# Sparse attention's rotated queries: a switch for turning them by transposing transfers, and the shift tables of a hand-tuned order redrawn

## The chip, the cores and the metric

The kernel runs on one core of a Trainium2 chip as one program. The metric is device time in microseconds. The kernel before takes 1057.03 us in the median of three runs (1057.02 to 1057.7). Five engines work side by side, each in its own fixed order of instructions: TensorE (PE) multiplies matrices into the banks of PSUM, VectorE (DVE), ScalarE (ACT) and GpSimd (POOL) compute, SyncE (SP) issues transfers. A semaphore holds an instruction until what it reads is there and what it overwrites is free; everything behind it on the same engine waits along.

## The reference

Two layers on 256 tokens of width 1024, each with a feed-forward half-step, a mixer and a second feed-forward half-step, each followed by a layer norm. The mixer of layer 0 is a hybrid of a gated delta rule and a state-space scan; that of layer 1 is sparse attention with compressed, selected and windowed keys.

```python
def reference(x, positions, ln_g, ln_b, ffn_w_in, ffn_w_out, hyb_w_in, ...):
    h = x
    for layer in range(DEPTH):
        i = layer // 2
        h = layer_norm(DEEPNORM_ALPHA * h + 0.5 * swiglu(h, ffn_w_in[layer, 0], ffn_w_out[layer, 0]), ...)
        if layer % 2 == 0:
            mix = hybrid_mixer(h, hyb_w_in[i], ...)
        else:
            mix = nsa_mixer(h, positions, nsa_w_in[i], ...)
        h = layer_norm(DEEPNORM_ALPHA * h + mix, ln_g[layer, 1], ln_b[layer, 1])
        h = layer_norm(DEEPNORM_ALPHA * h + 0.5 * swiglu(h, ffn_w_in[layer, 1], ffn_w_out[layer, 1]), ...)
    return h
```

In the sparse attention 16 heads of width 64 stand in two groups. The compressed branch uses the queries as projected; the selected and the windowed branch use `q_rot = partial_rope(q, positions)`, the rotated queries. Each branch is a masked softmax and a sum over values; three gates mix them, and an output projection follows.

## The kernel before

The work is cut into six stages (0 feed-forward, 1 hybrid mixer, 2 and 3 feed-forward, 4 sparse attention, 5 feed-forward). In the trace they reach, by the layer norms between them, to about 178, 403, 576, 751, 870 and 1056 us. The 256 tokens are two blocks b0 and b1 of 128.

*Products.* Weights come as float32 tiles `raw` and are split into a rounded part `whi` (by ACT, `whi<-raw`) and a remainder `wlo` (by DVE, `wlo<-raw,whi`); activations likewise into two halves of a tile `x`. `mm3` (L1139) then makes three fast products of each: hi hi, hi lo, lo hi. Projections go to PSUM tag `ps` (2 banks), transposes and wide feed-forward blocks to `mp` (2 banks), sums over a whole stage to `acc` (4 banks, one for each of two blocks and two column halves). A bank is free again when its last reader, a copy by ACT or DVE, is done.

*End of a stage.* `out_terms` (L1322) adds the terms of the output projection to the four `acc` banks. At the end of a stage the last five terms go block by block: first b0's two banks, then `then(b)`, which starts b0's layer norm, then b1's. The layer norm (L1274) reads each bank with `h<-acc,h`, takes statistics, scales and shifts in two pairs (`h<-h,lnmv,lng` and `h<-h,lnve,lnb`); the result is transposed on PE (`mp<-ident,h`) into the next stage's `x`.

*Stage 4.* `queries` (L2226) projects the queries of a group and block, turns the unrotated ones by `turn` (L868): ACT copies them apart into two 16-bit halves (`words<-q`), a transposing transfer on SP's queue turns these (`turned<-words`), ACT puts them together (`qT<-turned`). Then `rope` rotates q in place and PE transposes the result into a bank of `mp` (4 transposes for each of two groups and two blocks, `mp<-ident,q`), from where it is copied and split into `qs`. In the softmax P is normalised and turned on PE as well, four transposes to a bank (`mp<-ident,P`), and copied out (`PT<-mp`, by ACT or DVE). The products with the values (`mp<-PT,vtok` and, for the compressed branch, `mp<-arena,vbd`) give the attention's output, which is copied and split into a tile `x` for the output projection.

*Stage 5.* The feed-forward's projections by token (`ps<-x,whi` and `ps<-x,wlo`) alternate between the two `ps` banks; each is evicted by ACT and DVE into `sg` (`sg<-ps`, then `sg<-ps,sg`). Wide blocks, for which sums of weights `raw<-raw,raw` are formed on DVE, stand between them on `mp`.

*What sets the order.* Nothing issues directly: the functions add operations to a plan (`Plan.add`, L394), which a list scheduler (`Plan.order`, L546) places one by one by earliest start and then by priority. The scheduler also picks the engine of copies that may run on ACT or DVE, and the buffer of each tile. The priority is the operation's place in the program plus a shift. The shifts are the table `SHIFTS` (L51): for each stage and engine a list of runs (count, shift), handed to the stage's operations of that engine in program order (end of `K.run`, L2522). All instructions bear the line of the one helper that records them, L757 (L841 after the change).

Of the kernel before, what the change touches and what calls it, by code (L numbers as in the profile page):

```python
# [14 lines left out]
AF = mybir.ActivationFunctionType  # L15
# [37 lines left out]
        "tensor": [(18, -578), (1, 84), (2, -1851), (5, 0), (2, 407), (32, 0), (11, -1907), (2, 262), (32, 0), (22, 201), (5, 382), (5, 1394),  # L53
# [4 lines left out]
        "vector": [(2, -16), (1, 0), (4, 451), (1, 4), (1, -1802), (4, 0), (1, -739), (8, 0), (1, -2831), (3, 0), (8, 275), (1, 0), (2, 22), (7, 0),  # L58
            (1, -640), (1, 0), (1, -31), (12, -213), (2, 0), (18, -135), (1, -485), (1, -700), (4, 0), (12, -453), (6, 94), (3, 16), (1, -381),
            (2, -590), (5, 31), (3, 13), (4, 0), (6, -82), (1, -177), (3, -235), (2, 378), (4, -178), (10, -583)],  # L60
        "scalar": [(3, 756), (1, 0), (6, -699), (1, -20), (4, -2184), (2, 0), (2, -327), (6, -381), (1, -2057), (3, -1945), (1, -153), (12, 82),
            (2, 328), (1, -276), (1, -88), (1, -1), (2, -105), (2, -5), (4, 0), (1, -13), (2, -258), (16, 0), (1, -130), (2, 415), (1, 361),
            (1, -453), (12, 0), (2, 37), (14, 389), (1, -116), (1, 230), (2, 204), (4, -315), (1, -74), (7, -49), (1, -67), (2, -235), (5, -23),
            (2, 0), (10, -693)],
        "gpsimd": [(1, 451), (1, 0), (1, -714), (4, -48)],
        "sync": [(6, 0), (3, -1981), (1, -3772), (6, 0), (1, -85), (5, 1078), (2, 496), (1, 0), (56, 1116)],
    },
    1: {
        "tensor": [(218, 0), (26, -298), (75, 0), (2, 188), (1, 0), (1, 70), (1, 99), (2, 0), (4, -88), (4, 228), (1, 350), (2, -643), (29, 0),
# [10 lines left out]
        "vector": [(78, 0), (10, 241), (1, 3), (5, 408), (9, 40), (18, 0), (1, 273), (2, 293), (29, -903), (3, 392), (3, 504), (2, -456), (1, -320),  # L80
# [69 lines left out]
            (6, -110), (1, 231), (3, 362), (1, -167), (7, 0), (1, 315), (35, 0), (1, -864), (26, 0), (1, 124), (5, -449), (21, 0), (7, -1270),  # L150
            (3, -1446), (2, -1431), (1, -427), (7, -479)],
        "gpsimd": [(1, 315), (5, -62), (1, 2)],
        "sync": [(20, 0), (1, -123), (20, 0), (3, -484)],
    },
}

# [33 lines left out]
def H3(t, h):  # L190
    return t.rearrange("p (h t) -> p h t", h=h)
# [2434 lines left out]
```

## Time and profile before

| what | number |
|---|---|
| median of three runs | 1057.03 us |
| the profiled execution: its own time, its span | 1058.01 us, 1056.3 us |
| PE's idle time in the span | 12.57 us |
| of it in the windows 0-178, 178-403, 403-576, 576-751, 751-870, 870-1056.3 us | 1.90, 1.62, 0.00, 0.40, 1.07, 7.58 us |
| granted PE clock over the span | 0.999 |
| transposing transfers, transposes of rotated queries on PE | 39, 16 |

Matmuls overlap in the trace: an isolated 128x512 product shows about 0.39 us, while in a run their starts are 0.23 us apart. So a product that had to wait shows less idle time in its brackets than its start was put off. DVE is nearly as full as PE over the whole span, and nearly every copy or split of the kernel queues there or on ACT.

### The profile page before, as it was taken

The page shows a single profiled execution, that of the slowest core. Times are in us where ns is not written, and L with a number is a line of the kernel's source. Part 1 is how long each engine was busy: PE and PEld are TensorE (multiplying, and loading weights), DVE is VectorE, ACT ScalarE, POOL GpSimd, SP SyncE. Part 2 cuts the span into 40 slices and gives each one's busy share as a digit, 9 for nine tenths or more (in the row PEclk, how much of TensorE's full clock was granted, in tenths as well). Part 3 has the DMA queues.
Part 4 walks back from the last instruction along what each step waited for, and adds up shares of the span by engine and source line. Part 5 has one row for each costly group of instructions (what it writes and reads, how often), then busy time and mean ns, then how long its engine had stood idle before and what let it go on. Part 6 is the DMA issues. An engine that isn't in the chain of part 4 may idle for free.

```text
span 1056.3 us, 15912 instructions
## 1 busy us (share of the span) xinstructions
PE 1043.7 (99%) x5686; PEld 868.4 (82%) x5686; DVE 1006.7 (95%) x1430; ACT 772.0 (73%) x1155; POOL 84.9 (8%) x122
## 2 busy tenths in 40 slices
PE   9999999999999999999999999999999999999997
PEld 7888888899898888888888888788887778888886
DVE  6999999898999989999999999999988999999987
ACT  7676976379867966868876678687477976878880
POOL 1001000001000201110000200000010101000100
PEclk9999999999999999999999999999999999999999
DMA  9999986744962798999779845978664355689991
GB/s 322 296 285 269 286 287 193 222 114 114 203 198 72 227 283 235 285 283 264 275 229 316 236 160 179 261 253 278 212 202 148 110 184 136 202 232 248 297 276 40
DMA packets 185977, 235.35 MB, mean 223 GB/s; under 512 B 54365, under 2 KB 115498, under 8 KB 185898
## 3 DMA queue, kind: packets, MB, share of 16 engines
q1 hardware_dynamic: 176650, 216.51, 65.1%
q0 software_dynamic: 9248, 17.83, 9.8%
q8 instruction: 45, 0.74, 0.3%
q14 instruction: 34, 0.28, 0.1%
HBM read 221.30 MB, written 1.07 MB: 211 GB/s over the span
## 4 chain that ended last, share of the span: by engine, by line
PE 52%; DVE 14%; ACT 3%; issue 3%; DMA 3%; POOL 1%; DVEq 0%; ACTq 0%; POOLq 0%
PE ps L757 18%; PE acc L757 18%; PE mp L757 15%; DVE wlo L757 5%; DMA turned<-words 2%; DVE cv L757 2%; ACT whi L757 2%; DVE arena L757 1%; DVE raw L757 1%; DVE h L757 1%; DMA G<-rates 1%; DVE qs L757 1%; DVE sw L757 0%; POOL arena L757 0%; DVE y L757 0%
## 5 line engine op out<-in xcount | busy, mean ns | idle before, releaser
L757 DVE TENSOR_TENSOR wlo<-raw,whi 128x1024 fp32r<-128x1024 f32 (+2 forms) x447 | 522.2, 1207 | 5.5 <-ACT whi L757 4.9
L757 ACT ACTIVATE whi<-raw 128x1024 fp32r<-128x1024 f32 (+1 forms) x428 | 424.0, 1044 | 53.0 <-DVE raw L757 37.3
L757 PE MATMUL ps<-whi,x 128*128 128x512 f32 (+1 forms) x544 | 144.2, 384 | 0.2 <-DVE F L757 0.2
L757 PEld LDWEIGHTS ps<-whi,x 128*128 128x128 f32 x544 | 98.2, 188 | 18.2 <-DVE x L757 0.3
L757 DVE TENSOR_TENSOR raw<-raw,raw 128x1024 f32<-128x1024 f32 x94 | 112.1, 1218 | 0.3
L757 PE MATMUL ps<-x,whi 128*128 128x512 f32 (+2 forms) x464 | 104.6, 340 | 0.7 <-ACT cv L757 0.3
L757 PE MATMUL acc<-wlo,gh 128*128 128x512 f32 x253 | 99.1, 392 | 0.2 <-DVE wlo L757 0.2
L757 PE MATMUL acc<-whi,gl 128*128 128x512 f32 x253 | 97.9, 392 | 0.0
L757 PE MATMUL acc<-whi,gh 128*128 128x512 f32 x253 | 95.9, 392 | 0.0
L757 PEld LDWEIGHTS ps<-x,whi 128*128 128x128 f32 (+1 forms) x464 | 77.6, 187 | 10.2 <-DVE cv L757 0.6
L757 PE MATMUL acc<-whi,x 128*128 128x512 f32 x256 | 82.1, 404 | 1.0 <-DVE x L757 1.0
L757 PE MATMUL mp<-whi,x 128*128 128x512 f32 x288 | 78.3, 391 | 0.0
L757 PE MATMUL ps<-wlo,x 128*128 128x512 f32 (+1 forms) x272 | 77.7, 380 | 0.0
L757 PE MATMUL mp<-whi,fhi 128*128 128x512 f32 x192 | 75.1, 391 | 0.3 <-ACT whi L757 0.3
L757 PE MATMUL mp<-whi,flo 128*128 128x512 f32 x192 | 74.8, 390 | 0.0
L757 POOL DMA_DIRECT2D raw<-in_ffn_w_in_dram x34 | 41.1, 1216 | 337.6 <-DMA raw<-in_ffn_w_in_dram 205.1
L757 PE MATMUL ps<-x,wlo 128*128 128x256 f32 (+1 forms) x344 | 66.5, 284 | 0.0
L757 PE MATMUL acc<-whi,g 128*128 128x512 f32 x192 | 63.4, 392 | 0.0
L757 PEld LDWEIGHTS mp<-whi,x 128*128 128x128 f32 x288 | 53.2, 188 | 11.7 <-ACT su L757 0.6
L757 PE MATMUL mp<-wlo,fhi 128*128 128x512 f32 x192 | 59.4, 392 | 0.1
L757 PEld LDWEIGHTS acc<-whi,x 128*128 128x128 f32 x256 | 47.8, 190 | 11.6 <-DVE x L757 1.4
L757 PEld LDWEIGHTS ps<-wlo,x 128*128 128x128 f32 x272 | 49.5, 188 | 8.7 <-DVE wlo L757 0.2
(330 smaller groups left out, 1850.3 us busy)
## 6 DMA issues: line engine op xcount, KB each, us to landing
raw<-in_ffn_w_in_dram SPq DMA_DIRECT2D x162, 512.0 KB, 6.2
raw<-in_ffn_w_out_dram SPq DMA_DIRECT2D x88, 512.0 KB, 6.1
raw<-in_hyb_w_in_dram SPq DMA_DIRECT2D x44, 512.0 KB, 5.4
raw<-in_ffn_w_in_dram POOLq DMA_DIRECT2D x34, 512.0 KB, 9.1
raw<-in_ffn_w_in_dram SPq DMA_DIRECT2D x52, 256.0 KB, 4.7
raw<-in_hyb_w_out_dram SPq DMA_DIRECT2D x16, 512.0 KB, 4.4
raw<-in_nsa_w_in_dram SPq DMA_DIRECT2D x10, 512.0 KB, 5.4
raw<-in_nsa_cmp_w_dram SPq DMA_DIRECT2D x8, 512.0 KB, 3.9
```

The lines of the kernel that those rows point to most:

```text
L757: r = getattr(getattr(nc, eng), fn)(*[res(a) for a in args], **{k: res(a) for k, a in kw.items()})
```

## The change

New switches are added: `R_TURN` for turning the rotated queries by transfers instead of on PE, `P_TURN` for doing so with P, and `H_BANKS` for the bank tags of some projections. `turn` takes a list of sources as well. The tables in `SHIFTS` are replaced, for all six stages; they now hold more and shorter runs. All entries of `R_TURN` and `P_TURN` are 0, and those of `H_BANKS` name the tag that stood there before.

```diff
+R_TURN = (0, 0, 0, 0)
+P_TURN = (0,) * 24
+H_BANKS = ('ps', 'ps', 'ps', 'ps', 'ps', 'ps')
...
     def turn(self, out, src):
-        n = src.ids.size // P
+        n = out.ids.size // P
...
-        self.nc.scalar.activation(w, src.words(), AF.Copy)
+        parts = src if isinstance(src, list) else [src]
+        k = n // len(parts)
+        for j, part in enumerate(parts):
+            self.nc.scalar.activation(w[:, :, j * k:(j + 1) * k], part.words(), AF.Copy)
...
                 self.rope(H3(q[b][:, gs], 8), b, 8)
                 yield
-                pt = self.bank("mp")
-                for c in range(4):
-                    nc.tensor.transpose(pt[:, c * P:(c + 1) * P], q[b][:, g * 512 + c * P:g * 512 + (c + 1) * P], self.ident)
+                if R_TURN[2 * g + b]:
+                    pt = self.m4(512, "qr", "H")
+                    self.turn(H3(pt, 4), H3(q[b][:, gs], 4))
+                else:
+                    pt = self.bank("mp")
+                    for c in range(4):
+                        nc.tensor.transpose(pt[:, c * P:(c + 1) * P], q[b][:, g * 512 + c * P:g * 512 + (c + 1) * P], self.ident)
...
-                        self.copy(dst, pt)
+                        if P_TURN[g * 12 + half * 2 + r + (4 + half * 2 + r + kb if b else 0)]:
+                            self.turn(H3(dst, 4), [t[:, :, r, ks] for t in tiles])
+                        else:
+                            pt = self.bank("mp")
+                            for n in range(4):
+                                nc.tensor.transpose(pt[:, n * P:(n + 1) * P], tiles[n // nh][:, n % nh, r, ks], self.ident)
+                            self.copy(dst, pt)
```

The tables are long; these are the first runs of stage 5's PE table, new. Each pair is a count of instructions and the number added to the priority of each.

```diff
+        "tensor": [(45, 0), (1, 632), (4, 380), (3, 358), (1, 376), (8, 612), (34, 0), (1, 176), (1, 28), (10, 0), (3, 26), (15, 0), (12, 76),
```

The counts of stage 4's PE table sum to 671 before and to 655 now; the stage has 671 PE operations in both kernels. Stage 5's sums to 735 before (the rest has no shift) and to 777 now, all that the stage has.

The kernels hold the same instructions, apart from a few copies and splits whose engine the scheduler picks: 5233 on PE, 488 transfers issued by SP, 39 of them transposing, and PE's 16 transposes `mp<-ident,q`. The order differs from PE's row 145 on. PE's instructions stand by 2 to 7 rows elsewhere on average in stages 0 to 3, by 16 (at most 120) in stage 4 and by 11 (at most 95) in stage 5. Three places follow; the numbers in names tell tiles apart and differ between the kernels.

**The end of stage 4, PE.** Before, from the last product of the attention (`vbd`) on; x_1573 is the attention's output, acc_1630 and acc_1638 are b1's banks:

```order
L757 MATMUL mp_1676_9018<-arena_1486_7885,vbd_1557_8305 64x128 x8
L757 MATMUL acc_1630_8754<-wlo_1616_8674,x_1573_8407 128x512
L757 MATMUL acc_1630_8754<-whi_1600_8581,x_1573_8407 128x512
L757 MATMUL acc_1638_8824<-whi_1600_8581,x_1573_8407 128x512
L757 MATMUL acc_1638_8824<-wlo_1616_8674,x_1573_8407 128x512
L757 MATMUL acc_1638_8824<-whi_1600_8581,x_1573_8407 128x512
L757 MATMUL acc_1638_8824<-whi_1610_8616,x_1573_8407 128x512
L757 MATMUL acc_1638_8824<-wlo_1620_8690,x_1573_8407 128x512
L757 MATMUL acc_1630_8754<-whi_1610_8616,x_1573_8407 128x512
```

Now, from the same place; x_1581 is the attention's output, acc_1625 a bank of b0, acc_1621 and acc_1623 are b1's:

```order
L841 MATMUL mp_1676_9021<-PT_1671_9004,vtok_1468_7764 64x512
L841 MATMUL mp_1676_9021<-arena_1485_7882,vbd_1558_8319 64x128 x8
L841 MATMUL acc_1625_8736<-wlo_1639_8803,x_1581_8448 128x512
L841 MATMUL acc_1625_8736<-whi_1635_8792,x_1581_8448 128x512
L841 MATMUL acc_1621_8701<-whi_1587_8477,x_1581_8448 128x512
L841 MATMUL acc_1621_8701<-wlo_1591_8510,x_1581_8448 128x512
L841 MATMUL acc_1623_8710<-whi_1587_8477,x_1581_8448 128x512
L841 MATMUL acc_1623_8710<-wlo_1591_8510,x_1581_8448 128x512
```

Before, b0's last products stood ahead of the block of PT,vtok products that ends with `vbd`, and five products that read older parts of x stand between `vbd` and the first reader of the new part (whi_1610). Now b0's last two products come behind `vbd`, and the one after them (whi_1587) reads the new part.

**The end of stage 4, DVE.** Before, from b0's second read of its banks on; here ACT makes the first copy into x:

```order
L757 SCALAR_TENSOR_TENSOR h0_1661_8962<-acc_1609_8614,h0_1443_7633 128x512
L757 TENSOR_TENSOR wlo_1678_9025<-raw_1595_8553,whi_1673_9009 128x1024
L757 TENSOR_TENSOR wlo_1680_9032<-raw_1617_8676,whi_1677_9020 128x1024
L757 BN_STATS lnst_1664_8972<-h0_1661_8962 128x6
L757 BN_AGGR lnmv_1682_9045<-lnst_1664_8972 128x2
L757 TENSOR_SCALAR lnve_1683_9049<-lnmv_1682_9045 128x1
L757 SCALAR_TENSOR_TENSOR h0_1661_8962<-h0_1661_8962,lnmv_1682_9045,lng_1656_8931 128x512 x2
L757 TENSOR_TENSOR x_1573_8407<-mp_1676_9018,x_1573_8407 128x4x128
L757 SCALAR_TENSOR_TENSOR h0_1661_8962<-h0_1661_8962,lnve_1683_9049,lnb_1658_8937 128x512 x2
```

Now, from two splits ahead of the copy, which is a CAST on DVE:

```order
L841 TENSOR_TENSOR wlo_1681_9034<-raw_1579_8436,whi_1677_9024 128x1024
L841 TENSOR_TENSOR wlo_1683_9041<-raw_1592_8512,whi_1680_9032 128x1024
L841 CAST x_1581_8448<-mp_1676_9021 128x4x128
L841 SCALAR_TENSOR_TENSOR h0_1668_8994<-acc_1625_8736,h0_1443_7633 128x512
L841 TENSOR_TENSOR x_1581_8448<-mp_1676_9021,x_1581_8448 128x4x128
L841 BN_STATS lnst_1672_9007<-h0_1668_8994 128x6
L841 BN_AGGR lnmv_1686_9069<-lnst_1672_9007 128x2
L841 TENSOR_SCALAR lnve_1687_9072<-lnmv_1686_9069 128x1
L841 SCALAR_TENSOR_TENSOR h0_1668_8994<-h0_1668_8994,lnmv_1686_9069,lng_1658_8933 128x512 x2
L841 SCALAR_TENSOR_TENSOR h0_1668_8994<-h0_1668_8994,lnve_1687_9072,lnb_1659_8936 128x512 x2
```

The second read of b0's bank has moved from ahead of two splits to behind the CAST, the statistics come behind both conversions of x, and the conversion that stood between the two pairs of b0's layer norm is gone from there.

**Stage 5, the two ps banks.** PE before, from the last product of the projection ps_1737 to the first of ps_1757, two projections on:

```order
L757 MATMUL ps_1737_9345<-x_1694_9105,wlo_1729_9304 128x256
L757 MATMUL ps_1754_9422<-x_1694_9105,whi_1714_9248 128x512
L757 MATMUL mp_1743_9374<-whi_1744_9376,fhi_1711_9232 128x512
L757 MATMUL mp_1743_9374<-whi_1744_9376,flo_1712_9240 128x512
L757 MATMUL mp_1743_9374<-whi_1744_9376,fhi_1711_9232 128x512
L757 MATMUL mp_1743_9374<-whi_1744_9376,flo_1712_9240 128x512
L757 MATMUL mp_1743_9374<-wlo_1750_9405,fhi_1711_9232 128x512 x2
L757 MATMUL mp_1743_9374<-whi_1746_9385,fhi_1711_9232 128x512
L757 MATMUL mp_1743_9374<-whi_1746_9385,flo_1712_9240 128x512
L757 MATMUL ps_1757_9441<-x_1694_9105,whi_1721_9273 128x512
```

PE now, around the last products of ps_1751 and the first of ps_1759:

```order
L841 MATMUL ps_1751_9415<-x_1695_9110,wlo_1719_9266 128x256 x2
L841 MATMUL ps_1751_9415<-x_1695_9110,wlo_1722_9277 128x256 x3
L841 MATMUL mp_1734_9319<-wlo_1754_9435,fhi_1711_9233 128x512 x2
L841 MATMUL mp_1734_9319<-whi_1755_9441,fhi_1711_9233 128x512
L841 MATMUL mp_1734_9319<-whi_1755_9441,flo_1714_9244 128x512
L841 MATMUL mp_1734_9319<-whi_1755_9441,fhi_1711_9233 128x512
L841 MATMUL mp_1734_9319<-whi_1755_9441,flo_1714_9244 128x512
L841 MATMUL ps_1751_9415<-x_1695_9110,wlo_1722_9277 128x256
L841 MATMUL mp_1734_9319<-wlo_1756_9452,fhi_1711_9233 128x512 x2
L841 MATMUL ps_1759_9468<-x_1695_9110,whi_1724_9283 128x512 x4
```

DVE now, at the same place; ps_1747 is the projection before ps_1751 (its last product is 17 PE rows above that of ps_1751):

```order
L841 TENSOR_TENSOR wlo_1756_9452<-raw_1694_9106,whi_1755_9441 128x1024
L841 TENSOR_TENSOR raw_1704_9155<-raw_1704_9155,raw_1694_9106 128x1024
L841 TENSOR_TENSOR sg_1757_9460<-ps_1751_9415,sg_1757_9460 128x256
L841 TENSOR_TENSOR raw_1684_9043<-raw_1684_9043,raw_1726_9290 128x1024
L841 TENSOR_TENSOR raw_1694_9106<-raw_1694_9106,raw_1730_9303 128x1024
L841 TENSOR_TENSOR sg_1749_9401<-ps_1747_9375,sg_1749_9401 128x256
L841 TENSOR_TENSOR wlo_1762_9489<-raw_1684_9043,whi_1760_9476 128x1024
```

The new order evicts ps_1751 ahead of ps_1747, and ps_1759 starts two products behind the last one of ps_1751; before, nine products stood between a projection's end and the start of the one that takes its bank.

**Stage 4, the transposes of P.** Four of them fill a bank. PE before, for one half of b1's heads:

```order
L757 MATMUL mp_1586_8497<-ident_7_284,P_1567_8372 128x128 x2
L757 MATMUL mp_1586_8497<-ident_7_284,P_1571_8393 128x128 x2
L757 MATMUL ps_1581_8456<-whi_1526_8153,x_1454_7692 128x512
L757 MATMUL ps_1581_8456<-wlo_1529_8172,x_1454_7692 128x512
L757 MATMUL ps_1581_8456<-whi_1526_8153,x_1454_7692 128x512
L757 MATMUL ps_1581_8456<-whi_1531_8185,x_1454_7692 128x512
L757 MATMUL ps_1581_8456<-wlo_1534_8199,x_1454_7692 128x512
L757 MATMUL ps_1581_8456<-whi_1531_8185,x_1454_7692 128x512
L757 MATMUL mp_1587_8516<-ident_7_284,P_1567_8372 128x128 x2
L757 MATMUL mp_1587_8516<-ident_7_284,P_1571_8393 128x128 x2
L757 MATMUL mp_1588_8524<-ident_7_284,P_1567_8372 128x128 x2
L757 MATMUL mp_1588_8524<-ident_7_284,P_1571_8393 128x128 x2
```

PE now, for the same:

```order
L841 MATMUL ps_1583_8462<-kd1_1502_7979,qs01_1576_8422 128x256
L841 MATMUL mp_1595_8528<-ident_7_284,P_1577_8431 128x128
L841 MATMUL mp_1596_8531<-ident_7_284,P_1577_8431 128x128
L841 MATMUL mp_1595_8528<-ident_7_284,P_1577_8431 128x128
L841 MATMUL mp_1595_8528<-ident_7_284,P_1584_8465 128x128 x2
L841 MATMUL mp_1596_8531<-ident_7_284,P_1577_8431 128x128
L841 MATMUL mp_1596_8531<-ident_7_284,P_1584_8465 128x128 x2
L841 MATMUL mp_1600_8555<-ident_7_284,P_1577_8431 128x128 x2
L841 MATMUL mp_1600_8555<-ident_7_284,P_1584_8465 128x128 x2
L841 MATMUL mp_1602_8562<-ident_7_284,P_1577_8431 128x128 x2
L841 MATMUL mp_1602_8562<-ident_7_284,P_1584_8465 128x128 x2
L841 MATMUL ps_1604_8574<-kd0_1496_7958,qs01_1576_8422 128x256
```

Before, products of a projection (ps_1581) stand between the second group of four and the third, as further up between the first and the second; now sixteen transposes stand in a row.

More of the change, by code (lines that the diff above doesn't have):

```diff
@@ L61 @@
[L61 to L65, printed above, removed]
@@ new lines @@
+    3: {
+        "tensor": [(1, 3), (1, 4), (4, 0), (18, 7), (2, 76), (3, 0), (1, 6), (1, 21), (1, 22), (8, 24), (2, 39), (1, 0), (1, 41), (6, 0), (2, 70),
[9 rows of a table added]
+        "vector": [(1, -40), (2, -64), (2, 0), (1, 21), (1, 33), (2, 43), (5, 0), (1, 74), (1, 93), (1, -53), (1, 0), (1, -10), (1, 9), (1, 0),
[6 rows of a table added]
+        "scalar": [(6, -110), (2, 0), (2, 32), (1, 47), (1, 72), (1, -46), (1, -43), (2, 83), (1, 0), (1, 81), (1, 0), (1, -29), (1, -104), (1, -98),
[6 rows of a table added]
+        "gpsimd": [(1, -178), (1, -166)],
+        "sync": [(2, -213), (1, -205), (1, -211), (1, -205), (1, -202), (3, 0), (3, -164), (4, -161), (1, -266), (2, -265), (1, 0), (1, -278),
+            (1, -275), (1, 0), (1, -265), (2, -252), (4, -235), (2, -258), (4, 0), (2, -110), (2, -116), (1, -101), (6, 91), (2, -80), (1, -68),
+            (2, 0), (1, -78), (5, -68), (4, 0), (1, -85), (1, -71), (1, -91), (2, -89), (6, 0), (1, -55), (1, -29), (2, -28), (3, 0), (3, -106),
+            (1, -14)],
+    },
@@ new lines @@
+    5: {
+        "tensor": [(45, 0), (1, 632), (4, 380), (3, 358), (1, 376), (8, 612), (34, 0), (1, 176), (1, 28), (10, 0), (3, 26), (15, 0), (12, 76),
[7 rows of a table added]
+        "vector": [(1, 30), (6, 0), (1, 1), (1, 23), (1, 0), (1, 832), (2, 1013), (3, 0), (1, 103), (1, 143), (2, -31), (1, 16), (1, 176), (1, 122),
[4 rows of a table added]
+        "scalar": [(9, 3), (1, 400), (1, 106), (1, 430), (1, 0), (3, 1471), (1, -6), (8, 0), (1, -3), (5, 0), (2, -236), (4, 27), (3, 284),
+            (3, -171), (1, 116), (10, 0), (1, -450), (2, -603), (1, -607), (3, -192), (1, 281), (1, 182), (4, 0), (1, -210), (3, 0), (1, -11),
+            (2, -82), (1, -16), (41, 38), (1, 0), (1, 286), (1, 266), (3, 28), (9, -29), (1, 456), (4, 378), (7, 0), (2, 7), (2, 189), (2, 0),
+            (4, -57)],
+        "gpsimd": [(1, 65), (2, -278), (3, 315), (1, 81), (5, -183)],
+        "sync": [(1, 0), (27, 51), (4, -104), (4, -257), (6, 0), (1, -93), (2, -24), (5, 0), (1, -11), (1, 0), (1, 380), (1, 381), (20, 0), (1, 280),
+            (5, 214), (10, -57)],
@@ L1604, in z_gate_steps @@
             for b in range(2):
-                ps = self.bank("ps")
+                ps = self.bank(H_BANKS[4 + b])
                 for k in range(KD):
@@ L1961, in space @@
             vT = [H3(self.m4(1024, f"vT{n}"), 4) for n in range(2)]
-            yield from gdn_conv("v", [(8 + n, vT[n // 4][:, n % 4, :]) for n in range(8)])
+            yield from gdn_conv("v", [(8 + n, vT[n // 4][:, n % 4, :]) for n in range(8)], H_BANKS[:2])
             for b, d in enumerate(blk):
@@ L1992, in space @@
                     w = ws[0][e] if ws else self.these("x", self.unit_cols, w_in, 4112 + c * P, P)[0]
-                    ps = self.bank("ps")
+                    ps = self.bank(H_BANKS[2 + e])
                     yield from self.two_steps(x, w, ps)
@@ L2440, in attend @@
                 for r in range(2):
-                    tq = None
                     for kb in range(b + 1):
                         yield
-                        pt = self.bank("mp")
-                        for n in range(4):
-                            nc.tensor.transpose(pt[:, n * P:(n + 1) * P], tiles[n // nh][:, n % nh, r, kb * P:(kb + 1) * P], self.ident)
-                        if b == 0:
-                            if r == 0:
-                                tl = self.m4(1024, "PT", "Q")
-                            dst = tl[:, r * 512:(r + 1) * 512]
-                        else:
-                            if kb == 0:
-                                tl = self.m4(1024, "PT", "Q")
-                            dst = tl[:, kb * 512:(kb + 1) * 512]
-                        self.copy(dst, pt)
+                        ks = slice(kb * P, (kb + 1) * P)
+                        if b == 0 and r == 0 or b and kb == 0:
+                            tl = self.m4(1024, "PT", "Q")
+                        o = (kb if b else r) * 512
+                        dst = tl[:, o:o + 512]
+                        if P_TURN[g * 12 + half * 2 + r + (4 + half * 2 + r + kb if b else 0)]:
+                            self.turn(H3(dst, 4), [t[:, :, r, ks] for t in tiles])
+                        else:
+                            pt = self.bank("mp")
+                            for n in range(4):
+                                nc.tensor.transpose(pt[:, n * P:(n + 1) * P], tiles[n // nh][:, n % nh, r, ks], self.ident)
+                            self.copy(dst, pt)
                         PT[half, r, kb] = dst
```

61 lines of the change are left out of this document (25 added, 36 removed), and 180 rows, old and new, of the table SHIFTS.

## The prediction, made before the change was run

> **What bounds the kernel now.** I read the page's span and busy shares first, then the windows by stage, then the rows of TensorE's timeline that carry a wait. The page:
>
> ```profile
> span 1056.3 us, 15912 instructions
> ...
> PE 1043.7 (99%) x5686; PEld 868.4 (82%) x5686; DVE 1006.7 (95%) x1430; ACT 772.0 (73%) x1155; POOL 84.9 (8%) x122
> ```
>
> TensorE (PE) is the bound, with VectorE (DVE) close behind: an eviction or a layer norm that has to queue on DVE finds it busy 95% of the time. The windows, one row for a stage (stage 1, the hybrid mixer; stage 4, sparse attention; stage 5, the last feed-forward), say where PE has idle time:
>
> ```profile
> core 0: us, PE busy (x) PEld busy (x) DVE busy (x) ACT busy (x) POOL busy (x), PEclk, DMA share, GB/s
> 178.00:403.00 225.00, 223.38 (x1714) 197.43 (x1713) 210.45 (x431) 164.65 (x273) 18.55 (x28) 1.00 0.66 185
> 751.00:870.00 119.00, 117.93 (x782) 93.53 (x781) 110.71 (x228) 90.00 (x246) 13.80 (x27) 1.00 0.52 161
> 870.00:1056.30 186.30, 178.72 (x819) 147.55 (x818) 174.02 (x200) 129.42 (x156) 14.81 (x14) 0.99 0.74 206
> sum 1056.30, PE 1043.73 PEld 868.42 DVE 1006.65 ACT 772.04 POOL 84.90; mean PE 173.96 PEld 144.74 DVE 167.78 ACT 128.67 POOL 14.15
> ```
>
> PE idles 1056.30 - 1043.73 = 12.6 us. Of this 186.30 - 178.72 = 7.6 lie in stage 5, and nearly all of that behind PE's last product:
>
> ```profile
> 291.93 2.05 PE L757 MATMUL acc<-X,AT 64*64 64x32 f32 x64 [0.47 <-DVE X L757]
> ...
> 788.20 1.06 PE L757 MATMUL mp<-ident,P 128*128 128x128 f32 x8 [0.30 <-DVE P L757]
> ...
> 840.69 0.66 PE L757 MATMUL mp<-ident,P 128*128 128x128 f32 x4 [0.48 <-DVE arena L757]
> ...
> 1048.65 0.28 PE L757 MATMUL mp<-whi,gl 128*128 128x256 f32 x1
> ```
>
> That product starts at 1048.65 and the span ends at 1056.3, a tail whose order the change leaves as it is. Stage 1 idles 1.6 us and stage 4 1.1 us; the rows above the last (in brackets the idle time and who ended it) show the largest waits. Only work that PE no longer waits for, or new waits, can move the end, since its products are the same before and after: **everything is won or lost in waits of some tenths of a microsecond.** About 4 us of waits lie before the tail, some 6 if I add 0.16 to each, because products overlap (0.39 us each, started 0.23 apart, as a row below shows).
>
> **What the change is.** In its words the rotated queries are turned by transfers. The new switch for it, R_TURN, is zero in all four places. The order rows show PE with 16 transposes of q after the rope as before, and 39 transposing transfers both times. So what runs is the same work in another order: the SHIFTS tables are redrawn, in all six stages. Were the switches on, these rows would price it:
>
> ```profile
> L757 PE MATMUL mp<-ident,q 128*128 128x128 f32 x16 | 2.6, 275 | 0.0
> ...
> L757 ACT ACTIVATE words<-q 128x1024 uint16<-128x1024 uint16 x4 | 4.3, 1078 | 0.1
> ...
> L757 ACT ACTIVATE qT<-turned 128x1024 uint16<-128x1024 uint16 x4 | 5.5, 1380 | 0.0
> ```
>
> PE would lose at most 2.6 us and ScalarE (ACT) gain 4.3 + 5.5 = 9.8. They are off, so I cost this at 0. But stage 4's new table counts 655 of PE's instructions, sixteen fewer than the 671 that the stage has and that the old table counts. Behind the first of the sixteen transposes its numbers fall on instructions up to sixteen places off. I read it as numbers drawn for the form with the switches on. Stages 0 to 3 and 5 have tables that fit.
>
> **Term A, end of stage 4: +1.2 us (0 to 2.3).** Here is how the stage ended before:
>
> ```profile
> 868.05 1.04 PE L757 MATMUL mp<-arena,vbd 128*64 128x128 f32 x16
> 869.02 0.50 PE L757 MATMUL acc<-wlo,x 128*128 128x512 f32 x1
> ...
> 873.65 1.04 PE L757 MATMUL mp<-ident,h 128*128 128x128 f32 x8
> ```
> ```profile
> 869.14 0.60 ACT L757 ACTIVATE x<-mp 128x512 fp32r<-128x512 f32 x1 [3.45 <-PE mp L757]
> ```
> ```profile
> 868.14 0.69 DVE L757 BATCH_NORM_STATS2 lnst<-h 128x6 f32<-128x512 f32 x1
> ...
> 869.17 1.41 DVE L757 SCALAR_TENSOR_TENSOR h<-h,lnmv,lng 128x512 f32<-128x512 f32 x2
> 870.50 0.69 DVE L757 TENSOR_TENSOR x<-mp,x 128x512 fp32r<-128x512 f32 x1
> 871.10 1.41 DVE L757 SCALAR_TENSOR_TENSOR h<-h,lnve,lnb 128x512 f32<-128x512 f32 x2
> 872.42 1.22 DVE L757 TENSOR_TENSOR wlo<-raw,whi 128x1024 fp32r<-128x1024 f32 x1
> ```
>
> After the last attention product (vbd, 868.05) five products that need no new input cover the copy of its result into x: the copy ends at 869.14 + 0.60 = 869.74, and the sixth product starts at about 869.02 + 5 x 0.23 = 870.2. The h0 transposes at 873.65 find h ready (872.5). In the new order two products stand between vbd and the first reader of x, the copy is a DVE cast behind four weight splits (1.22 each), and b0's last product, which h0 <- acc waits for, comes after vbd and no longer before the 3.5 us of PT,vtok products. With DVE free at 869.14 the cast ends at 869.83 against a reader at 869.48: with a hand-off about 0.5 of wait. The second half of x (DVE third in line, 0.60 apart) is done near 871.05, its reader due near 870.9: 0.2. Layer norm goes on for 0.7 + 0.25 + 1.4 + 1.4 (statistics, small operations, two pairs) to 874.7, the first transposes at PE's thirteenth product after that are due at 874.0 and want the first half, near 874.2: 0.2. The next stage's x then has its two conversions with less PE work beside them: 0.3. Sum 1.2. If the cast has to wait out one split the first term grows by 1.1; if x is free early, nothing of this shows.
>
> **Term B, stage 5, the two ps banks: +0.85 us (0 to 2).** The eviction of one projection takes an ACT and a DVE step:
>
> ```profile
> 900.66 0.39 ACT L757 ACTIVATE sg<-ps 128x256 f32<-128x256 f32 x1 [1.13 <-PE ps L757]
> ```
> ```profile
> 901.20 0.42 DVE L757 TENSOR_TENSOR sg<-ps,sg 128x256 f32<-128x256 f32 x1
> ```
> ```profile
> 902.32 2.00 PE L757 MATMUL ps<-x,whi 128*128 128x512 f32 x8
> ```
>
> From ACT's start to DVE's end it is 901.62 - 900.66 = 0.96 us; products start (2.00 - 0.39) / 7 = 0.23 apart. In the new DVE order the eviction of ps_1747, long complete, stands behind that of ps_1751, so the projection ps_1759 takes the bank of ps_1751, whose last product lies two products (0.46) ahead of it. 0.28 for that product plus 0.96 and hand-offs, less 0.12 + 0.46, is 0.75; a raw <- raw of about 1.2 us ahead on DVE may add: 0.85. Before, nine products stood at that place. Later ps_1810 meets the same with its su <- ps copy two products ahead: +0.4 (0 to 0.6).
>
> **Term C, transposes of P: +0.9 us (0 to 1.2).** The copies out of the two mp banks, and the densest stretch of these transposes now:
>
> ```profile
> L757 ACT ACTIVATE PT<-mp 128x512 f32<-128x512 f32 x16 | 9.1, 598 | 2.0 <-PE mp L757 1.8
> ```
> ```profile
> 860.18 1.03 PE L757 MATMUL mp<-ident,P 128*128 128x128 f32 x8
> 860.97 0.71 PE L757 MATMUL acc<-whi,x 128*128 128x512 f32 x2
> ...
> 861.75 1.04 PE L757 MATMUL mp<-ident,P 128*128 128x128 f32 x8
> ```
>
> Eight transposes fill both banks in 0.8 us and 0.78 us of products follow, as long as a copy. The new order puts sixteen in a row: the third four needs the first bank back, three transposes (0.33) after it was filled, against 0.27 + 0.60 (somewhat more where DVE copies) and hand-offs; the fourth four waits for the other copy. About 0.6 + 0.3.
>
> **What goes: -1.8 us (-6 to 0).** The eight transposes at 788.20 now stand in fours with two other rows between: the 0.30 there (0.46 by starts) goes. Of the rest of stage 4 I let as much go again, and 0.9 of stages 1 to 3, whose tables are now drawn in finer runs. Their waits (0.47 at 291.93 the largest) hang on chains of ACT and DVE that the order can cover but not shorten.
>
> **Queueing that I can't place: +1.4 us (0 to 7).** In stage 4 PE's rows move by 16 places on average, up to 120, with numbers meant for other instructions, and DVE there is at 110.71 of 119 us. No row prices a misplaced eviction before it happens. The nearest is stage 4's own 1.1 us of idle time (some 1.6 with overlaps), so I take about that; the upper end is five such stretches.
>
> **Sum:** 1.2 + 0.85 + 0.4 + 0.9 - 1.8 + 1.4 = +2.95. The profiled execution took 1058.01 (span 1056.3 and 1.7 around it) and would become 1060.96. The median shown is 1057.03, about 1 us below it; the same step gives **1060.0**.
>
> **Rivals.** (1) *The new waits are paid by old ones* (28%): A to C are covered because DVE runs ahead of PE there, and the sum stays within 2.1 us, 1055 to 1059. For it speaks that 4 us of idle time is small anyway; against it that each place has two products of cover where five to nine stood. (2) *Faster* (16%): the finer tables of stages 1 to 3 take away the waits on X, cv and x, and stage 4 those at 788 and 840. It decides where A to C cost under 1.5 together while over 4 of the 6 us go: 1053 to 1054.9. (3) *Stage 4's table out of step costs much* (11%): each of its 24 PT copies or 16 softmax blocks late by 0.4 gives 6 to 10 us, 1063 to 1067. (4) *The clock* (1%): the windows show PEclk 1.00 in every stage but the last, whose 0.99 holds the idle tail; 0.01 more of 186.3 us would cost 1.9 us, giving 1062. The Trainium skill ("TensorE: Matmul & The Clock Gate", section "A second HAM failure mode: psum-queue depth-cycling") says that short idle times between groups of products that cycle through PSUM banks can swing the clock between half and full. By that rule terms B and C could cost more than their waits; the waits at 788 and 840 lie in a window with 1.00 granted, so the trace so far speaks against it. That the change turns the queries by transfers has no chance of its own, since the rows of the new order still hold the transposes.
>
> **How the numbers follow.** Forecast +2.1 to +6: 44%. With (3) and (4) that makes slower 56%, within 0.2% (2.1 us, what a measurement of this kernel can tell from no change) 28%, faster 16%. The range leaves out about a tenth at each side: half of (2)'s gain at the low end, 1054.5, and most of (3) at the high, 1066.5.
>
> **What would show it.** A: brackets on acc <- whi,x just behind mp <- arena,vbd, and on mp <- ident,h. B: a bracket on ps <- x,whi near 905 to 920 naming sg. C: sixteen mp <- ident,P with brackets naming PT. Queueing: PE's idle time in stage 4's window above 1.1 us by more than A and C. I am wrong if stage 4 and 5 together idle no more than now, or if stages 1 to 3 give back over 2 us.

## The result, and the profile after

The changed kernel takes 1071.72 us in the median of four runs (1069.73 to 1075.82), before 1057.37 (1057.02 to 1058.4): **1.0143 of the time before, 95% interval 1.0127 to 1.0159.** Slower, as forecast, but by some 14 us and not by 3, and above the range's upper end of 1066.5. The profiled execution was the slowest of its runs, 1075.82 us. Its page:

```profile
span 1074.1 us, 15926 instructions
PE 1050.9 (98%) x5686; PEld 870.8 (81%) x5686; DVE 1008.2 (94%) x1425; ACT 772.1 (72%) x1158; POOL 85.7 (8%) x124
```

The work is the same; PE is busy 7 us longer for it, and idle for longer. To show where, the windows below run between three marks: the last transposes of h (`mp<-ident,h` of b1) behind stage 3, those behind stage 4, and PE's last product. Columns as in the prediction: bounds, length, busy time of PE, PEld, DVE, ACT, POOL, granted clock. Before:

```profile
0.00:764.40 764.40, 760.48 (x4173) 639.37 (x4173) 735.29 (x1026) 558.47 (x765) 58.14 (x84) 1.00 0.79 236
764.40:885.80 121.40, 120.33 (x775) 94.43 (x774) 111.88 (x227) 92.82 (x248) 15.28 (x28) 1.00 0.52 161
885.80:1048.70 162.90, 162.69 (x744) 134.60 (x742) 155.07 (x169) 120.75 (x144) 10.55 (x10) 1.00 0.77 212
```

After, and below it three short windows in it:

```profile
0.00:769.00 769.00, 762.95 (x4188) 642.43 (x4189) 736.35 (x1027) 562.24 (x772) 59.89 (x84) 1.00 0.79 235
769.00:895.70 126.70, 120.42 (x760) 93.95 (x758) 110.97 (x221) 90.19 (x243) 11.96 (x28) 0.97 0.45 142
895.70:1066.50 170.80, 167.27 (x744) 134.43 (x741) 156.69 (x169) 119.70 (x144) 12.97 (x11) 0.99 0.73 213
830.10:836.90 6.80, 5.84 (x28) 5.85 (x28) 5.97 (x13) 5.30 (x13) 2.72 (x7) 0.50 0.20 39
301.10:304.50 3.40, 3.40 (x9) 2.64 (x9) 3.27 (x7) 1.36 (x2) 0.25 (x1) 0.50 0.40 139
939.30:942.70 3.40, 3.40 (x8) 2.72 (x9) 3.40 (x5) 3.40 (x5) 0.91 (x1) 0.51 1.11 217
```

Stages 0 to 3 end 4.6 us later, stage 4 takes 5.3 more, stage 5 7.9 more; the tail is 7.6 us both times. By cause: PE's idle time ahead of its last product was 3.9 + 1.1 + 0.2 = 5.2 us and is 6.1 + 6.3 + 3.5 = 15.9, so 10.7 more. And PE was granted half its clock for 3.4, 6.8 and 3.4 us, which before did not happen ahead of the tail; half of 13.6 us is 6.8 us of work lost at most (PE was idle for 1 us of them, which both sums count). 10.7 + 6.8 = 17.5 of the 17.8 us by which the span grew. (In the rows for single stages some work has moved over a mark.)

The largest single loss, in PE's timeline:

```profile
824.73 0.28 PE L841 MATMUL ps<-kd,qs 128*128 128x256 f32 x1
828.28 0.44 PE L841 MATMUL mp<-ident,P 128*128 128x128 f32 x2 [3.27 <-ACT P L841]
829.07 0.88 PE L841 MATMUL mp<-ident,P 128*128 128x128 f32 x6 [0.35 <-ACT P L841]
831.06 1.97 PE L841 MATMUL mp<-ident,P 128*128 128x128 f32 x8 [1.11 <-DVE PT L841]
```

These are the sixteen transposes of term C. Their brackets sum to 4.7 us, and the half clock of the window at 830.1 follows: eight transposes that took 1.03 us at 860.18 before take 1.97. ACT's timeline in the same stretch:

```profile
823.41 0.50 ACT L841 ACTIVATE P<-acc,arena 128x256 f32<-128x256 f32 x1
...
827.00 0.55 ACT L841 ACTIVATE P<-acc,arena 128x256 f32<-128x256 f32 x1
...
827.64 3.43 ACT L841 ACTIVATE P<-P,arena 128x256 f32<-128x256 f32 x8
```

ACT does sixteen exponentials (some 0.45 us apart, the last ten in a row, a short accumulator read with each), and only then normalises P (`P<-P`), which PE wants. Before, at the same place, ACT normalised the first half's P ahead of the last four exponentials, and the transposes of P stood between projections (`ps<-whi,x` and `ps<-wlo,x`):

```profile
816.88 1.77 ACT L757 ACTIVATE P<-P,arena 128x256 f32<-128x256 f32 x4
818.48 0.54 ACT L757 ACTIVATE P<-acc,arena 128x256 f32<-128x256 f32 x1
```
```profile
818.39 0.49 PE L757 MATMUL mp<-ident,P 128*128 128x128 f32 x3
...
820.57 0.60 PE L757 MATMUL mp<-ident,P 128*128 128x128 f32 x4
...
822.41 1.32 PE L757 MATMUL mp<-ident,P 128*128 128x128 f32 x8
```

DVE, in the changed kernel, shows no idle time from 823 to 833 us. The copy that gives the second eight transposes their bank stands behind its own queue:

```profile
826.92 1.22 DVE L841 TENSOR_TENSOR P<-P,arena 128x1024 f32<-128x1024 f32 x1
...
829.18 1.22 DVE L841 TENSOR_TENSOR wlo<-raw,whi 128x1024 fp32r<-128x1024 f32 x1
830.32 0.68 DVE L841 COPY PT<-mp 128x512 f32<-128x512 f32 x1
```

So the wait of 3.27 us is PE's longest, but with DVE's order as it is the second eight would have waited without it too: the chain of work that ended last runs through DVE here, not through ACT. Terms A and B left these rows:

```profile
879.24 1.02 PE L841 MATMUL acc<-whi,x 128*128 128x512 f32 x2
...
880.56 0.40 PE L841 MATMUL acc<-wlo,x 128*128 128x512 f32 x1
881.02 0.73 PE L841 MATMUL acc<-whi,x 128*128 128x512 f32 x2
...
884.13 0.63 PE L841 MATMUL mp<-ident,h 128*128 128x128 f32 x4
...
927.26 2.11 PE L841 MATMUL ps<-x,whi 128*128 128x512 f32 x8 [0.73 <-DVE sg L841]
...
937.82 1.19 PE L841 MATMUL acc<-whi,g 128*128 128x512 f32 x4 [1.44 <-ACT whi L841]
...
956.78 0.50 PE L841 MATMUL ps<-whi,fhi 128*128 128x512 f32 x1 [0.23 <-ACT su L841]
```

A: two products in 1.02 where two in a row take 0.62, and a start 0.23 late at 881.02; none at the transposes of h. B: 0.73 on sg, and 0.23 on su. The 1.44 on `whi` at 937.82 stood in no term.

### The profile page after: what moved, and what is told of

The parts are those of the page before. It is cut to its first block, busy times and chain, and to the rows that moved or that the text cites. A ratio compares the mean times of both kernels' runs of the same rounds, so it can differ in the third digit from the quotient of the medians.

```text
span 1074.1 us, 15926 instructions
## 1 busy us (share of the span) xinstructions
PE 1050.9 (98%) x5686; PEld 870.8 (81%) x5686; DVE 1008.2 (94%) x1425; ACT 772.1 (72%) x1158; POOL 85.7 (8%) x124
## 4 chain that ended last, share of the span: by engine, by line
PE 54%; DVE 4%; DMA 2%; ACT 1%; issue 1%; POOL 0%; DVEq 0%; ACTq 0%; POOLq 0%
PE ps L841 19%; PE acc L841 19%; PE mp L841 17%; DMA raw<-in_ffn_w_in_dram 2%; ACT whi L841 1%; DVE arena L841 1%; DVE raw L841 1%; DVE wlo L841 0%; DVE qs L841 0%; DVE h L841 0%; DVE x L841 0%; POOL lnve L841 0%; DVE F L841 0%; DVE vg L841 0%; DVE P L841 0%
```

## The experiments

The theories, of which C took shape on the way: **M**, the loss is a table out of step, since its numbers fall on other instructions than they were drawn for; **L**, it is the sum of separate places; **C**, a table holds only for the whole schedule that it was drawn with; **K**, lost clock that follows from waits. Times are medians, ratios to the kernel before on the same chip with their intervals.

### Whole tables exchanged

Six of these seven kernels take one or more stages' entries of `SHIFTS` from before; three set the switch.

```diff
 SHIFTS = {
...
-    4: {"tensor": [...], ...},    # new
+    4: {"tensor": [...], ...},    # of before
...
-R_TURN = (0, 0, 0, 0)
+R_TURN = (1, 1, 1, 1)
```

Stage 4's table of before:

> The changed kernel with stage 4's table of before (PE, DVE, ACT, POOL, SP lists), all else as changed. Theory L (the loss is local: in the profile of the changed kernel stage 4 holds waits of 3.3, 0.35 and 1.1 us on the transposes of P at 828 to 831 us and then 6.8 us at half clock, worth 4.7 + 3.4 = 8 us; stage 5 holds waits of its own): 1071.7 - 8, so 1062 to 1066, with stage 5's waits near 927 and 938 still there. Rival H (stage 5's waits are handed over from stage 4's bad end): both go, 1056 to 1059.

Stage 5's:

> The changed kernel with stage 5's table of before, all else as changed. Theory L: stage 5 gives back its waits (some 3.5 us of brackets between 927 and 959) and the 1.7 us that its 3.4 us at half clock cost, so 1065 to 1068, with the wait on ACT's P at about 828 and the half clock behind it unchanged. Rival H: stage 5's waits stay or come elsewhere, 1070 to 1073.

Both:

> The changed kernel with the tables of before in stages 4 and 5: what is left of the change is the new tables of stages 0 to 3 alone. Theory L: no half clock before the tail and the stages 1 to 3 as in the changed kernel, which reach the same point 4.6 us later than before in its profile (1.7 of it half clock at 301): 1058 to 1062. Rival S (stages 0 to 3 gained by their finer tables, the profile's shift is only work moved over a stage's border): 1053 to 1057.

All tables new and the switch on:

> The changed kernel with R_TURN = (1, 1, 1, 1): the rotated queries are turned by four more transfers, as the change's words say, PE has 16 transposes fewer, ACT eight copies more, and stage 4's table of 655 PE entries fits its 655 instructions. Theory M (the loss in stage 4 comes from a table that is out of step): the wait before the transposes of P and the half clock go, 1060 to 1064. Rival O (the order of the table is bad for the chip by itself: sixteen transposes of P still stand in a row there): the wait stays, 1068 to 1073.

The next three expectations were written with the results of these four known. The switch on, stages 0 to 3 of before:

> The changed kernel with R_TURN = (1, 1, 1, 1) and the tables of before in stages 0 to 3: the turning by transfers and the new tables of stages 4 and 5 alone, which is what the change's words say. Adding up by stages (before's 764.4 us to the end of stage 3, then 118.9 + 163.5 + 7.8 us as in x4_turn_on): a span of 1054.6, a time of 1056, within 0.2% of before. Theory C (a stage's table holds only behind the stages it was drawn behind): stage 4 and 5 take 10 us or more longer, 1066 or more.

The switch on, all tables of before:

> The changed kernel with R_TURN = (1, 1, 1, 1) and all tables of before: the turning by transfers by itself, with nothing redrawn. By its work alone (2.6 us less on PE at most, 9.8 us more on ACT): 1055 to 1060. Theory C: the old table of stage 4 meets other instructions, 1066 to 1090.

The switch off, stages 0 to 3 of before:

> The changed kernel (R_TURN 0) with the tables of before in stages 0 to 3: the new tables of stages 4 and 5 alone. If the loss belongs to these two tables without the turning, as in the changed kernel: stage 4 about 126, stage 5 about 170 us, 1067 to 1073. Theory C in its strong form (every mix comes out differently): outside of that, either way.

Measured (the last three columns from the marks described above, in each profile):

| kernel | tables 0-3, 4, 5; turns | time, us | ratio | end of stage 3 | stage 4 | stage 5 |
|---|---|---|---|---|---|---|
| before | old, old, old; off | 1057.3 | 1 | 764.4 | 121.4 | 162.9 |
| changed | new, new, new; off | 1071.7 | 1.0143 (1.0127 to 1.0159) | 769.0 | 126.7 | 170.8 |
| x4 | new, new, new; **on** | 1059.2 | 1.0017 (1.0007 to 1.0026) | 767.6 | 118.9 | 163.5 |
| x2 | new, new, old; off | 1066.8 | 1.0086 (1.0058 to 1.0114) | 769.3 | 125.3 | 163.1 |
| x8 | old, new, new; on | 1079.2 | 1.0195 (1.0180 to 1.0210) | 766.1 | 132.7 | 169.9 |
| x1 | new, old, new; off | 1085.6 | 1.0290 (1.0247 to 1.0332) | 762.9 | 137.6 | 174.7 |
| x10 | old, new, new; off | 1088.2 | 1.0284 (1.0267 to 1.0301) | 767.2 | 134.9 | 174.8 |
| x3 | new, old, old; off | 1091.8 | 1.0325 (1.0307 to 1.0343) | 767.4 | 135.1 | 180.5 |
| x9 | old, old, old; on | 1095.5 | 1.0354 (1.0339 to 1.0370) | 762.5 | 155.8 | 167.4 |

With the switch on, as the change's words have it, the new tables give almost the time of before, 0.17% above it: with all four turns on PE gone (2.6 us of busy time at most) nothing is won, but 12 us of loss do not come either. Stage 4 then takes 118.9 us. This is a little better than theory M asked for (1060 to 1064), and since the code is the same but for the switch, it shows that the loss comes from running these tables without the transfers. (The changed code with all tables of before and the switch off was not run.) **Theory L falls.** The very table of stage 4 that gives 121.4 us behind the old stages 0 to 3 gives 135.1 and 137.6 behind the new ones (x3, x1), and the new one that gives 118.9 behind new stages gives 132.7 behind the old (x8). x8 is the clearest: by adding up stages it should have taken 1056 us, and it takes 1079. My expectations for x1 and x3 (1062 to 1066, 1058 to 1062) were off by some 20 and 30 us for that reason; x9 and x10 came out above the 1066 to 1090 of theory C and the 1067 to 1073 of adding up. One mix goes against the strong form of C: x2, where stage 5's old table behind the new stage 4 takes 163.1 us, as at home, and gives back 7.7 us of the changed kernel's profile; its time of 1066.8 us lies in the 1065 to 1068 that theory L had named. So stage 5's loss hangs on its table and not on a bad hand-over alone.

### The same number for the same instruction

```diff
+                    self.turned.append(len(self.plan.ops))
                     for c in range(4):
                         nc.tensor.transpose(...)
...
-                mine = iter([op for op in ops if op.eng == eng])
+                mine = []
+                for op in ops:
+                    if op.idx in self.turned:
+                        mine += [None] * {"scalar": 2, "sync": 1}.get(eng, 0)
+                    if op.eng == eng and not any(0 <= op.idx - k < 4 for k in self.turned):
+                        mine.append(op)
```

> The changed kernel with R_TURN still 0, but stage 4's table handed out as if it were 1: the sixteen transposes of rotated queries on PE take no entry, and where the transfers would stand ACT passes over two entries and SP over one, so that every other instruction gets the number that it has with the turns on. Theory M (a number for the wrong instruction is what costs): 1060 to 1064, no wait of 3 us ahead of the transposes of P, no half clock near 830. Rival C (the table holds only for the whole schedule it was drawn with, so that the transposes on PE and their PSUM banks are enough to upset it): 1066 to 1073, with waits of over 3 us in sum in stage 4.

1076.23 us, ratio 1.0175 (1.0151 to 1.0199), stage 4 127.9 us, stage 5 171.0. **Theory M falls too**, though I had built the forecast's reading of the table on it. Every instruction but the sixteen transposes, which have no shift, has the number drawn for it, and the kernel is no faster than the changed one. So what the table misses is not its place in the list. That it misses the transfers themselves follows from x4: with four transposes for each block on PE and a bank of `mp` between, the scheduler puts out another order. Whether shifts of their own for the sixteen transposes would mend it was not tried. The profile shows the 3.3 us at P gone and others in their place (DVE on PT 2.3 us in four waits, ACT on PT 1.2, ACT on P 0.9 in stage 4), and half clock for 3.41 us at 828.7 and again at 839.0. Theory C's sum of over 3 us came; its time, 1066 to 1073, was too low.

How the same place looks in x4, PE's timeline:

```profile
824.57 0.87 PE L841 MATMUL mp<-ident,P 128*128 128x128 f32 x6 [0.36 <-ACT P L841]
826.10 1.43 PE L841 MATMUL mp<-ident,P 128*128 128x128 f32 x8 [0.66 <-ACT PT L841]
828.08 1.26 PE L841 MATMUL mp<-ident,P 128*128 128x128 f32 x8 [0.54 <-DVE PT L841]
```

There too sixteen transposes stand in a row, and more. The second and third eight wait 0.66 and 0.54 us for their banks, 1.2 in sum, near the 0.9 of term C; but the scores whose exponentials P needs start at 810.3, 42.7 us into the stage, with projections between them until 821.7. In the changed kernel their first part comes at 44.5 us, but the last eight products start at 52.3 to 55.4, the last projection starts at 54.6 and the last product of all at 55.7, and from 56.0 to 59.3 PE has nothing to do.

### What the wait at P consists of

```diff
+        early = {6537, 6538, 6539, 6540}      # P<-P of the first half, on ACT
+        moved = [x for i, x in zip(placed, order) if i in early]
+        at = placed.index(6536) + 1           # behind the reciprocal's product
+        return order[:at] + moved + [x for i, x in zip(placed[at:], order[at:]) if i not in early]
```

> The changed kernel with four instructions moved on ACT alone: the normalising of the first half's P (P <- P, four), which in the changed order stands behind the eight exponentials of the second half, goes to right behind the reciprocal that it needs, ahead of the last four of these exponentials. In the profile of the changed kernel the reciprocal's product is done at 825.86 us and the first of the four starts at 827.64. Theory E (the 3.3 us that PE waits there are ACT's order: the transposes of P wait for ACT, not for their PSUM banks): that wait falls to some 1.5 us, the time by 1.5 to 4 us (what the half clock behind it gives back included), so 1068 to 1071 where x13_again gives about 1072 to 1073. Rival F (the banks, or DVE's share of the normalising, or ACT's total work are late next, as I had priced it): the wait only moves to the next transposes, within 1 us of x13_again.

> The changed kernel on the same chip, beside x12_scale_first: 1070 to 1075, with the wait of 3.3 us at about 828.

x12 takes 1074.16 us, ratio 1.0159 (1.0134 to 1.0184), the changed kernel beside it 1071.68, ratio 1.0130 (1.0112 to 1.0149): no gain, so E's 1068 to 1071 is missed, and by the medians 2.5 us more where F said within 1, with intervals that overlap. PE in x12, and DVE:

```profile
824.35 0.44 PE L846 MATMUL mp<-ident,P 128*128 128x128 f32 x2 [1.49 <-ACT P L846]
...
826.02 0.76 PE L846 MATMUL mp<-ident,P 128*128 128x128 f32 x5 [0.54 <-DVE P L846]
830.55 1.97 PE L846 MATMUL mp<-ident,P 128*128 128x128 f32 x8 [3.76 <-DVE PT L846]
```
```profile
827.53 0.28 DVE L846 TENSOR_TENSOR arena<-arena,arena 128x120 f32<-128x120 f32 x1 [1.56 <-ACT arena L846]
...
828.67 1.22 DVE L846 TENSOR_TENSOR wlo<-raw,whi 128x1024 fp32r<-128x1024 f32 x1
829.80 0.69 DVE L846 COPY PT<-mp 128x512 f32<-128x512 f32 x1
```

Both theories had a half of it. The wait on ACT's P falls from 3.27 to 1.49 us, where E said 1.5, so that wait was ACT's order (the four now stand ahead of the last four exponentials, as they do before). But the next eight transposes then wait 3.76 us for the copy out of their bank, as F said: that copy stands on DVE behind a product that waits 1.56 us for ACT (`arena`, behind the exponentials moved back), a cast and a split. From the end of stage 3 to the second eight transposes it is 63.7 us in x12 and 62.1 in x13. The four instructions were in the wrong place, and a better place for them alone is worth nothing here, because DVE's queue holds the next transposes all the same.

### The clock

```diff
+            if op.idx == 6542:                # the first of the sixteen transposes
+                pt, (_, kd, qs) = args[0].t.view(), ops[6708].args[:3]
+                order += [("tensor", "matmul", (pt[:, :256], kd, qs), dict(start=True, stop=True))] * 26
```

> The changed kernel with 26 products more (128x256, kd by qs, into the PSUM bank that the transposes of P overwrite next; 26 x 0.12 = 3.1 us) where PE waits 3.3 us for P. Theory K (the 6.8 us at half clock behind 830 us follow from PE's idle time, and cost 3.4 us by themselves): no half clock there or 3.4 us of it only, 1.7 to 3.4 us faster than the changed kernel, 1068 to 1070, though PE has more to do. Rival N (the half clock has another cause): the half clock stays, 1071 to 1073.

> As x6_fill_products, with 28 transposes of the identity (128x128, 28 x 0.11 = 3.1 us) in place of the products. If transposes count as work for the clock as products do: as there, 1068 to 1070. If they don't: the half clock at 830 stays, 1071 to 1073.

x6 takes 1072.03 us (1071.03 to 1073.07), ratio 1.0141 (1.0121 to 1.0161); x6b 1074.39, ratio 1.0157 (1.0132 to 1.0181) (1072.28 to 1074.57 in three executions; a fourth ran at 0.555 of the clock from end to end, took 1753.79, and is the one that was profiled). x6's profile:

```profile
824.36 3.27 PE L844 MATMUL mp<-kd,qs 128*128 128x256 f32 x26
827.80 0.44 PE L844 MATMUL mp<-ident,P 128*128 128x128 f32 x2 [0.17 <-ACT P L844]
828.59 0.88 PE L844 MATMUL mp<-ident,P 128*128 128x128 f32 x6 [0.35 <-ACT P L844]
830.58 1.97 PE L844 MATMUL mp<-ident,P 128*128 128x128 f32 x8 [1.11 <-DVE PT L844]
```

With the gap filled the half clock comes still, but for 3.41 us (830.5 to 833.9) where the changed kernel has 6.83 in three profiles. That much is in K's words; but the time, 1072.0, is in rival N's range and not in K's, and stage 4's 125.6 us stand beside 125.8 to 126.7 in the changed kernel's three profiles. Nor did the filling take all idle time away: 0.17 + 0.35 + 1.11 = 1.6 us of waits are left just ahead of the half clock. So x6 doesn't decide between K and N, and x6b doesn't either; what ties the half clock to idle time is the count over all profiles in the last section.

The changed kernel once more:

> The changed kernel once more, five rounds, for the clock: its time less the time lost to the granted clock (one minus the mean clock, times the span). Theory K: its runs differ by the number of 3.4 us episodes at half clock, so that the time less the lost time is steadier, 1063 to 1068, while the lost time goes from 4 to 10 us; before loses about 2 us, all of it behind PE's last product. Rival: the lost time is as in before, and the runs differ by waits.

1073.94 us, ratio 1.0153 (1.0132 to 1.0173). Over its thirteen executions in three sessions the changed kernel takes 1068.74 to 1077.74 us. The time lost to the granted clock (one minus its mean, given to 0.1%, times the span) is 4.3 to 9.7 us, 7 on average; before it is 1.1 to 3.2, in its profile all of it in the tail. Less the lost time the changed kernel takes 1063 to 1069, 1066 on average, and before about 1056. So roughly 10 us of the loss are waits and some 5 the clock. The rival (lost time as in before) is out; but the time less the lost time still spreads over 6 us, so it is not only the clock in which the runs differ.

```diff
+        late = {2676, 2677, 2681, 2682, 2689, 2714, 2715, 2716, 2717}   # ps<-x,whi
+        moved = [x for i, x in zip(placed, order) if i in late]
+        at = placed.index(2153)               # in the middle of the small products
```

> x4_turn_on with nine of stage 1's projections (ps <- x,whi, 2 us in all) moved 3 us forward on PE, into the middle of a stretch of 192 small products (64x32) after which four of five profiles of the new stage 1 show 3.41 us at half clock, near 301 us. Theory K2 (a long stretch of small products brings the half clock though PE counts as busy): none near 301, and 1.7 us faster than x4_turn_on, 1057 to 1058. Rival: the half clock comes as before or the projections wait for their banks, 1059 to 1060.

1064.7 us (1058.75 to 1066.68), ratio 1.0061 (1.004 to 1.0081): slower than x4. Three of nine executions have a clock of 0.998 and 1058.75 to 1060.58 us; the profile is of one of these and has no half clock at 301, as K2 expects. The other six have 0.991 or 0.992, so some 6 to 7 us more lost, at places that no profile shows. The median is outside both forecasts: moving the projections did not bring x4 down, and what lowered the clock in those six stays open.

## Why the prediction was wrong

**The bound and the direction** were right: PE's products are the same, only waits decide, and the new waits outweigh the old. That the switch is off, and that stage 4's table was drawn with it on, was read rightly from its count of 655; x4, where the table fits, takes 1059.2.

**Term A** (1.2): 0.4 + 0.2 us of late starts at 879 to 881 and none at the transposes of h. The mechanism is there for half of the price; x's copy found DVE free.

**Term B** (0.85 and 0.4): 0.73 on sg, about 1.0 by starts, and 0.23 on su, 0.4 by starts. Right in place and size.

**Term C** (0.9, at most 1.2) is the step that failed. It asked how fast two banks can be emptied, "0.27 + 0.60" and hand-offs, and took P for granted. The wait was 4.7 us, 3.6 of them for P itself, and half clock behind it for another 3.4 us of work. In the prediction the projections that used to stand between these transposes were counted as cover for a copy of 0.6 us. Before, they stood there from 817.6 to 822.4 us, while ACT did the last exponentials and normalised P: they were cover for the end of ACT's sixteen exponentials (0.45 us each, 7 us in all) and for the normalising. The price for the banks was sound: 1.2 us in x4, with P there in time, and 0.41 to 1.11 in the changed kernel's three profiles. x12 shows ACT's order as the cause of the wait for P, and DVE's queue as what holds the transposes next.

**What goes** (-1.8): the wait at 788 went. Waits on F (0.63) and arena (0.44) came at 787 and 794, and stages 0 to 3 did not win 0.9: in the changed kernel's profile they end 4.6 us later, 1.7 of it clock. Across the runs with new tables 0 to 3 their end is at 762.9 to 770.5, with old ones at 762.5 to 767.2, so the new ones bring no gain, and a loss that these profiles don't settle.

**Queueing** (+1.4, up to 7): the runs put about 10 us to waits in all, of which the three named places have some 6 to 7; the largest unnamed one is the 1.44 us on `whi` at 937.82. I had sized this by the idle time of a kernel whose order was in balance, which says nothing of one whose order isn't.

**The rivals.** The clock, which the sum put at nothing and to which I gave 1% because the windows of before show 1.00, took some 5 us of the 14. Those windows hold waits of half a microsecond and said nothing about one of three. The Trainium skill ("TensorE: Matmul & The Clock Gate", section "What's actually happening") gives a window of about 3.4 us and a clock that is either full or half; ahead of the tail the episodes here last 3.41, 6.83, 10.24 or 13.65 us at 0.50, so the traces agree but for one: x6b's execution of 1753.79 us was granted 0.555 for most of its span, which is neither full nor half. Rival 3, stage 4's table out of step at 6 to 10 us, had the nearest time and a cause that x5 refutes as I put it.

## What to carry to other kernels

A list of priorities tuned against a scheduler is a property of the whole schedule: change the work anywhere, or exchange one stage's part, and the rest of the list may no longer be tuned (here 1.9 to 3.5% for five mixes out of six, 0.9% for the sixth). So switch and tables go in or out together, and a forecast for a table that was drawn for other work starts from a loss of that order and not from the waits one can name. When an order takes cover away from an instruction, price everything that the instruction waits for, the producer of its operand first, then what the other engines hold next, and then ask whether the idle time is enough to cost clock as well.

## What the runs showed of the hardware

In the fifteen profiles other than x6b's, each half clock ahead of the tail begins a whole number of windows of 3.413 us behind the first full clock of its execution, and lasts one to four of them (32 times: 18, 11, 2 and 1). The changed kernel's windows around the sixteen transposes, with the granted clock in the third column from the end:

```profile
823.30:826.71 3.41, 1.71 (x10) 1.27 (x8) 3.38 (x8) 3.41 (x17) 0.00 (x0) 1.00 0.63 205
826.71:830.12 3.41, 1.31 (x8) 0.84 (x8) 3.41 (x8) 3.41 (x12) 0.00 (x0) 1.00 0.01 3
830.12:833.53 3.41, 2.47 (x12) 2.48 (x13) 3.25 (x6) 3.38 (x7) 1.43 (x4) 0.50 0.00 0
833.53:836.95 3.42, 3.42 (x18) 3.42 (x18) 2.71 (x8) 1.95 (x8) 1.29 (x4) 0.50 0.40 77
```

PE is idle for 1.70 us of the first, and the clock stays full; for 2.10 of the second, and half clock follows; for 0.94 of the third, and half clock goes on; in the fourth it is busy, and full clock returns. Counted over all windows at full clock outside stage 1's stretch below: half clock follows all 17 with 1.88 us of idle time or more, 7 of the 49 with 0.9 to 1.87, and none with less. So some 2 us within one window were enough, in one wait or several, and by where the windows fall the same waits can cost clock or not.

It halved also where PE had hardly been idle: behind this stretch of stage 1 in the new order, 192 products of 64x32 with 0.17 us of idle time in this profile,

```profile
294.58 2.06 PE L841 MATMUL acc<-T,Y 64*64 64x32 f32 x64
296.47 1.91 PE L841 MATMUL acc<-Y,T 64*64 64x32 f32 x58
298.54 2.15 PE L841 MATMUL acc<-X,AT 64*64 64x32 f32 x64 [0.17 <-DVE X L841]
300.48 0.45 PE L841 MATMUL acc<-Y,T 64*64 64x32 f32 x6
300.86 3.91 PE L841 MATMUL ps<-x,whi 128*128 128x512 f32 x9
```

nine products then take 3.91 us, in x1's profile, without the half clock, 2.33. Eight of ten profiles with that order have it, none of four with the order of before. That small products don't hold the clock is argued from this and not shown. The length of the stretch doesn't decide: it is 6.3 us here, with the half clock, 5.9 to 6.2 in the order of before, and 6.9 and 6.6 in x1 and x5, which have the new order and no half clock. A rival is left as well: nine of the ten, x1 and x5 among them, also hold 0.17 to 1.58 us of idle time in the third group that the profile puts down to no engine. And x7, which split the stretch, had no half clock there in its profile but lost more clock elsewhere in most of its runs.
